# Storing the last tile's 128 results as a column instead of a transposed row

## The chip, the cores and the metric

The kernel runs on one core of a Trainium2 chip. The metric is the device time of one execution in microseconds (us). A second source is the profile: one execution recorded by the hardware profiler, whose span runs from the first to the last recorded instruction.

## The reference

```python
def setup_inputs():
    return {"x": np.random.randn(64, 256, 8192).astype(np.float32)}

def reference(x):
    return np.mean(x, axis=2)
```

The mean over the last axis: 64 x 256 = 16384 rows of 8192 floats each, one result per row. 537 MB are read, 64 KB are written.

## The kernel before, in words

The 16384 rows are seen as 128 tiles of 128 rows (one row to a partition). The first 126 tiles are taken in 63 pairs: partition p of a pair holds two neighbouring rows, 64 KB, in one of three buffers (`bufs`). SyncE's queue (SP) issues all loads: three at the start, then in a loop each as soon as its buffer is free (L108). For each pair VectorE (DVE) sums the first row of each partition into a column of `res0` (L138), and ScalarE (ACT) sums the second row into a column of `res1` (L177).

The last two tiles, T0 and T1, come one by one into the buffer that the loop would use next. T0 is one load (L117); VectorE sums one half, ScalarE the other, and VectorE adds the two halves into `last0` (L145). T1 comes in six chunks of falling size (L119: 4096, 2048, 1024, 512, 256 and 256 columns). Four chunks are halved between VectorE (L148) and ScalarE (L177); VectorE folds the fifth (L153). The sixth lies in a tile `fin` next to the ten partial sums, and one last fold on VectorE (L153, the function `folded`) adds chunk and partial sums, scales by 1/8192 and leaves the 128 finished results of T1 in `last1`, one float on each of 128 partitions. That fold increments `dve_sem` to 3.

The order on each engine is written out by hand, with semaphores between engines. At the end:

- TensorE (PE) transposes `res0` and `res1` through an identity matrix into PSUM (L209, L210). ScalarE copies both, scaled, into `outsb` (L181), and SP stores it (L123).
- TensorE transposes `last0` into `psum_row0`, one row of 128 (L213). ScalarE copies it, scaled, to `row0` (L181, `from_psum`), and SP stores that row of 512 bytes (L126).
- TensorE transposes `last1` into `psum_row1` (L213). VectorE copies it to `row1` (L171), and SP stores this row (L126).
- SP waits for the three stores (L130).

`cp_sem` counts the copies out of PSUM, `pe_sem` the transposes; SP waits for `cp_sem` at 2, 3 and 4 before the three stores.

Of the kernel before, what the change touches and what calls it, by code (L numbers as in the profile page):

```python
# [11 lines left out]
def bass_global_avg_pool_1d_kernel(  # L12
# [4 lines left out]
    P = 128  # L17
# [15 lines left out]
    T0, T1 = 2 * NB, 2 * NB + 1  # L33
    out_flat = out.rearrange("b c -> (b c)")
    out_pairs = out_flat.rearrange("(g q) -> g q", q=2 * P)
    out_tiles = out_flat.rearrange("(t p) -> t p", p=P)
# [11 lines left out]
    with ExitStack() as ctx:  # L48
        sb = lambda n, s: ctx.enter_context(nc.sbuf_tensor(n, s, F32))
        ps = lambda n, s: ctx.enter_context(nc.psum_tensor(n, s, F32))  # L50
        sem = lambda n: ctx.enter_context(nc.semaphore(n))
        half = sb("half", [P, 2])
        last = [sb(f"last{j}", [P, 1]) for j in range(2)]
# [6 lines left out]
        ident = sb("ident", [P, P])  # L60
        outsb = sb("outsb", [NB, 2 * P])
        fin = sb("fin", [P, NFIN])
        added = sb("added", [P, NFIN // 2])
        row = [sb(f"row{j}", [1, P]) for j in range(2)]
        psum = [ps(f"psum{j}", [NB, P]) for j in range(2)]
        psum_row = [ps(f"psum_row{j}", [1, P]) for j in range(2)]
        dve_sem = sem("dve_sem")
        act_sem = sem("act_sem")
        ident_sem = sem("ident_sem")
        pe_sem = sem("pe_sem")  # L70
        cp_sem = sem("cp_sem")
        tile_sem = sem("tile_sem")
        out_sems = [sem(f"out_sem{i}") for i in range(3)]
# [9 lines left out]
        def chunk(c):  # L83
            if c == NCH - 1:
                return fin[:, 0 : ch[c]]
            return tail[:, L + offs[c] : L + offs[c] + ch[c]]


        eng = nc.gpsimd
# [14 lines left out]
        eng = nc.sync  # L104
# [16 lines left out]
            ).then_inc(ch_sems[c], 16)  # L121
        eng.wait_ge(cp_sem, 2)
        eng.dma_start(out_pairs[0:NB, :], outsb[:, :]).then_inc(out_sems[0], 16)  # L123
        for j in range(2):
            eng.wait_ge(cp_sem, 3 + j)
            eng.dma_start(out_tiles[T0 + j : T0 + j + 1, :], row[j][:, :]).then_inc(  # L126
                out_sems[1 + j], 16
            )
        for s in out_sems:
            eng.wait_ge(s, 16)  # L130

# [1 line left out]
        eng = nc.vector  # L133
# [18 lines left out]
        def folded(ap, n, to, scale, done):  # L152
            eng.tensor_tensor_reduce(  # L153
                added[:, 0 : n // 2],
                ap[:, 0 : n // 2],
                ap[:, n // 2 : n],
                scale=scale,
                scalar=0.0,
                op0=ADD,
                op1=ADD,  # L160
                accum_out=to,
            ).then_inc(done, 1)
# [4 lines left out]
        eng.wait_ge(pd_sem, NS + 1)  # L167
        eng.wait_ge(ch_sems[NCH - 1], 16)  # L168
        folded(fin, NFIN, last[1][:], inv, dve_sem)
        eng.wait_ge(pe_sem, 4)  # L170
        eng.tensor_copy(row[1][:, :], psum_row[1][:, :]).then_inc(cp_sem, 1)  # L171


        eng = nc.scalar

        def summed(ap, to, done):
            eng.activation(ap, ap, COPY, accum_out=to).then_inc(done, 1)  # L177

        def from_psum(n, dst, src):
            eng.wait_ge(pe_sem, n)  # L180
            eng.activation(dst, src, COPY, scale=inv).then_inc(cp_sem, 1)  # L181
# [16 lines left out]
        for c in range(NS):  # L198
            eng.wait_ge(ch_sems[c], 16)
            summed(chunk(c)[:, ch[c] // 2 :], part(NS + 1 + c), pa_sem)  # L200
            if c == 0:
                from_psum(3, row[0][:, :], psum_row[0][:, :])


        eng = nc.tensor
# [2 lines left out]
            eng.wait_ge(free_sems[b], 2 * NT)  # L208
        eng.transpose(psum[0][:, :], res[0][:, :], ident[:, :]).then_inc(pe_sem, 1)  # L209
        eng.transpose(psum[1][:, :], res[1][:, :], ident[:, :]).then_inc(pe_sem, 1)  # L210
        for j in range(2):
            eng.wait_ge(dve_sem, 2 + j)
            eng.transpose(psum_row[j][:, :], last[j][:, :], ident[:, :]).then_inc(  # L213
                pe_sem, 1
            )


# [26 lines left out]
```

## Time and profile before

| what | value |
| --- | --- |
| time, median of 3 runs | 1244.41 us (1244.21 to 1244.49) |
| the profiled execution's own time | 1244.37 us |
| its span | 1243.0 us |
| busy: VectorE, ScalarE, TensorE | 557.2, 458.8, 1.4 us |
| DMA queue, share of 16 engines' span | 99.8% |
| read from HBM, mean rate | 536.87 MB, 432 GB/s |
| VectorE's copy of `psum_row1` (L171) | 0.279 us |
| one transpose into `psum_row` (L213) | 0.372 us |

The profiled execution took 1.37 us more than its span; that time lies outside the recorded instructions. Busy times are sums over instructions, and engines work side by side, so they do not add up to the span. The chain that ended last names at each moment what the end was waiting for. Waits of SP are listed on their own.

### The profile page before, as it was taken

Reading aid. Unit: us, or ns where it says so; the run is one execution under the profiler, and the core shown is the slowest. Engines: PE = TensorE matmul, PEld = TensorE weight load, DVE = VectorE, ACT = ScalarE, POOL = GpSimd, SP = SyncE. Lnnn points to the kernel's source line nnn. Section 1 sums busy time; section 2 is a strip of 40 time slices with the busy share of each in tenths; the row PEclk is TensorE's granted clock in tenths of the full one; section 3 lists DMA queues with packets and bytes.
Section 4 is the critical chain, followed back from the end, with each engine's and each line's share of the span. In section 5 each row is a group of like instructions: output and inputs, shape, how many; then the busy total and the mean of one; then the engine's idle time right before and its main releaser. Section 6 shows DMA issues by size and latency. Waiting matters only on the chain.

```text
span 1243.0 us, 887 instructions
## 1 busy us (share of the span) xinstructions
PE 1.4 (0%) x4; PEld 0.4 (0%) x4; DVE 557.2 (45%) x74; ACT 458.8 (37%) x141; POOL 0.7 (0%) x7
## 2 busy tenths in 40 slices
PE   0000000000000000000000000000000000000000
PEld 0000000000000000000000000000000000000000
DVE  2354453543535435344353453544535435354356
ACT  2243242432424424334243342433424324244245
POOL 0000000000000000000000000000000000000000
DMA  9999999999999999999999999999999999999998
GB/s 405 439 439 439 405 439 439 439 439 439 439 422 422 439 439 439 439 439 432 411 439 439 439 439 439 439 426 418 439 439 439 439 439 434 415 432 439 439 439 373
DMA packets 10156, 536.94 MB, mean 432 GB/s; under 512 B 1131, under 2 KB 1452, under 8 KB 1708
## 3 DMA queue, kind: packets, MB, share of 16 engines
q1 hardware_dynamic: 10156, 536.94, 99.8%
HBM read 536.87 MB, written 0.07 MB: 432 GB/s over the span
## 4 chain that ended last, share of the span: by engine, by line
DMA 84%; DVE 15%; issue 0%; SPq 0%; DVEq 0%; PE 0%
DMA buf<-in_x_dram 84%; DVE res L138 15%; SPq L108 0%; DVEq L138 0%; DVE fin L148 0%; SPq L119 0%; DVE added L153 0%; PE psum_row L213 0%; SPq L117 0%; DVE row L171 0%; DVEq L168 0%; DVE fin L153 0%; DVE last L153 0%
## 5 line engine op out<-in xcount | busy, mean ns | idle before, releaser
L138 DVE TENSOR_REDUCE res<-buf 128x8192 f32 x63 | 547.2, 8686 | 682.7 <-DMA buf<-in_x_dram 682.7
L177 ACT ACTIVATE buf<-buf 128x8192 f32<-128x8192 f32 (+2 forms) x68 | 450.5, 6625 | 778.8 <-DMA buf<-in_x_dram 778.7
L177 ACT ACTIVATION_READ_ACCUMULATOR buf<-buf (+1 forms) x68 | 12.6, 186 | 0.0
L142 DVE TENSOR_REDUCE half<-buf 128x1 f32<-128x4096 f32 x1 | 4.4, 4419 | 0.9 <-DMA buf<-in_x_dram 0.9
L148 DVE TENSOR_REDUCE fin<-buf 128x1 f32<-128x2048 f32 (+3 forms) x4 | 4.6, 1153 | 0.3 <-DMA buf<-in_x_dram 0.2
L209 PE MATMUL psum<-ident,res 128*63 128x128 f32 x1 | 0.4, 442 | 1230.1 <-DVE res L138 1230.1
L184 ACT ACT_TABLE_LOAD x1 | 1.3, 1283 | 0.7 <-PEq L229 0.7
L181 ACT ACTIVATE outsb<-psum 63x128 f32<-63x128 f32 x2 | 0.5, 278 | 2.2 <-PE psum L209 2.2
L213 PE MATMUL psum_row<-ident,last 128*1 128x128 f32 x2 | 0.7, 372 | 10.1 <-DVE last L153 5.2
L209 PEld LDWEIGHTS psum<-ident,res 128*63 128x63 f32 x1 | 0.2, 181 | 1230.1 <-issue 1230.1
L171 DVE COPY row<-psum_row 1x128 f32<-1x128 f32 x1 | 0.3, 279 | 0.5 <-PE psum_row L213 0.5
L210 PE MATMUL psum<-ident,res 128*63 128x128 f32 x1 | 0.4, 417 | 0.0
L153 DVE CUSTOM_DVE_ANT_0 added<-fin 128x133 f32<-128x133 f32 x1 | 0.3, 299 | 0.1
L153 DVE CUSTOM_DVE_ANT_0 added<-buf 128x128 f32<-128x128 f32 x1 | 0.3, 293 | 0.0
L93 POOL TENSOR_SCALAR_AFFINE_SELECT ident<-ident 128x128 f32<-128x128 f32 x1 | 0.3, 292 | 0.2 <-POOL ident L91 0.2
L181 ACT ACTIVATE row<-psum_row 1x128 f32<-1x128 f32 x1 | 0.2, 249 | 0.0
L210 PEld LDWEIGHTS psum<-ident,res 128*63 128x63 f32 x1 | 0.2, 231 | 0.0
L184 ACT ACTIVATE warm<-ident 128x1 f32<-128x1 f32 x1 | 0.2, 203 | 0.0
L91 POOL MEMSET ident<- 128x128 f32 x1 | 0.2, 204 | 0.0
L145 DVE TENSOR_REDUCE last<-half 128x1 f32<-128x2 f32 x1 | 0.2, 155 | 0.1
L213 PEld LDWEIGHTS psum_row<-ident,last 128*1 128x1 f32 x2 | 0.2, 79 | 10.8 <-DVE last L153 5.5
L229 POOL MEMSET const-bfloat16-1.0<- 128x1 bf16 x1 | 0.1, 101 | 0.0
(6 smaller groups left out, 0.6 us busy)
## 6 DMA issues: line engine op xcount, KB each, us to landing
buf<-in_x_dram SPq DMA_DIRECT2D x1, 4096.0 KB, 39.5
buf<-in_x_dram SPq DMA_DIRECT2D x1, 2048.0 KB, 43.9
buf<-in_x_dram SPq DMA_DIRECT2D x1, 1024.0 KB, 45.9
buf<-in_x_dram SPq DMA_DIRECT2D x63, 49.0
buf<-in_x_dram SPq DMA_DIRECT2D x1, 512.0 KB, 46.7
buf<-in_x_dram SPq DMA_DIRECT2D x1, 256.0 KB, 46.9
buf<-in_x_dram SPq DMA_DIRECT2D x1, 128.0 KB, 46.8
fin<-in_x_dram SPq DMA_DIRECT2D x1, 128.0 KB, 46.6
```

The source lines that it names most:

```text
L93: eng.affine_select(out=ident[:], in_=ident[:], compare_op=mybir.AluOpType.not_equal, fill=1.0, base=0, pattern=[[-1, P]], channel_multipl ...
L138: eng.tensor_reduce(res[0][:, bass.ds(NBUF * i + b, 1)], bufs[b][:, 0:L], X, ADD).then_inc(free_sems[b], 1)
L142: eng.tensor_reduce(half[:, 0:1], tile0[:, 0:H], X, ADD).then_inc(dve_sem, 1)
L148: eng.tensor_reduce(part(c), chunk(c)[:, 0 : ch[c] // 2], X, ADD).then_inc(pd_sem, 1)
L153: eng.tensor_tensor_reduce(added[:, 0 : n // 2], ap[:, 0 : n // 2], ap[:, n // 2 : n], scale=scale, scalar=0.0, op0=ADD, op1=ADD, accum_ou ...
L171: eng.tensor_copy(row[1][:, :], psum_row[1][:, :]).then_inc(cp_sem, 1)
L177: eng.activation(ap, ap, COPY, accum_out=to).then_inc(done, 1)
L181: eng.activation(dst, src, COPY, scale=inv).then_inc(cp_sem, 1)
L184: eng.activation(warm[:], ident[:, 0:1], COPY)
L209: eng.transpose(psum[0][:, :], res[0][:, :], ident[:, :]).then_inc(pe_sem, 1)
L210: eng.transpose(psum[1][:, :], res[1][:, :], ident[:, :]).then_inc(pe_sem, 1)
L213: eng.transpose(psum_row[j][:, :], last[j][:, :], ident[:, :]).then_inc(pe_sem, 1)
```

## The change

The 128 results of T1 are no longer transposed. SP waits for the last fold (`dve_sem` at 3) and stores `last1` as it lies: 128 partitions of one float each go to 128 consecutive floats of the output, in one DMA. The transpose of `last1`, the PSUM tile and the row tile for it, and VectorE's copy go. T0 is handled as before.

```diff
-        row = [sb(f"row{j}", [1, P]) for j in range(2)]
+        row = sb("row", [1, P])
-        psum_row = [ps(f"psum_row{j}", [1, P]) for j in range(2)]
+        psum_row = ps("psum_row", [1, P])
...
         eng.wait_ge(cp_sem, 2)
         eng.dma_start(out_pairs[0:NB, :], outsb[:, :]).then_inc(out_sems[0], 16)
-        for j in range(2):
-            eng.wait_ge(cp_sem, 3 + j)
-            eng.dma_start(out_tiles[T0 + j : T0 + j + 1, :], row[j][:, :]).then_inc(
-                out_sems[1 + j], 16
-            )
+        eng.wait_ge(cp_sem, 3)
+        eng.dma_start(out_tiles[T0 : T0 + 1, :], row[:, :]).then_inc(out_sems[1], 16)
+
+        eng.wait_ge(dve_sem, 3)
+        eng.dma_start(
+            out_tiles[T1].rearrange("(p o) -> p o", o=1), last[1][:]
+        ).then_inc(out_sems[2], 16)
         for s in out_sems:
             eng.wait_ge(s, 16)
...
         folded(fin, NFIN, last[1][:], inv, dve_sem)
-        eng.wait_ge(pe_sem, 4)
-        eng.tensor_copy(row[1][:, :], psum_row[1][:, :]).then_inc(cp_sem, 1)
...
-                from_psum(3, row[0][:, :], psum_row[0][:, :])
+                from_psum(3, row[:, :], psum_row[:, :])
...
-        for j in range(2):
-            eng.wait_ge(dve_sem, 2 + j)
-            eng.transpose(psum_row[j][:, :], last[j][:, :], ident[:, :]).then_inc(
-                pe_sem, 1
-            )
+        eng.wait_ge(dve_sem, 2)
+        eng.transpose(psum_row[:, :], last[0][:, :], ident[:, :]).then_inc(pe_sem, 1)
```

## The prediction

> **What bounds the kernel now.** The page comes first: the span, the DMA rows, and the chain that ended last.
>
> ```profile
> span 1243.0 us, 887 instructions
> ...
> DMA packets 10156, 536.94 MB, mean 432 GB/s; under 512 B 1131, under 2 KB 1452, under 8 KB 1708
> ...
> q1 hardware_dynamic: 10156, 536.94, 99.8%
> ...
> DMA 84%; DVE 15%; issue 0%; SPq 0%; DVEq 0%; PE 0%
> ```
>
> The one DMA queue is busy for 99.8% of the span and moves 432 GB/s: loading x is the kernel. The change touches no load, so it acts only after the last load has landed. The chain of waits from the end of VectorE's last fold on is:
>
> ```profile
> 1241.15 0.02 DVE last L153
> 1241.17 0.04 issue
> 1241.21 0.39 PE psum_row L213
> 1241.60 0.02 issue
> 1241.62 0.28 DVE row L171
> ```
>
> It is a strict sequence. VectorE's last fold ends at 1241.17, TensorE transposes from 1241.21 to 1241.60, VectorE copies from 1241.62 to 1241.90. The timeline and the waits of the SP queue give the rest:
>
> ```profile
> 1241.93 0.23 SPq L126 DMA_DIRECT2D out_dram<-row  x1
> ```
>
> ```profile
> SPq L130 <- DMA out_dram<-row: 0.8, 1, 0.8
> ```
>
> The store of the last row is issued from 1241.93 to 1242.16, and SP then waits 0.8 us for it: 1243.0 − 1241.93 = 1.07 us from the start of the issue to the end of the span. Where those 1.07 us lie, and how a DMA of 128 rows looks when the queue is empty, is seen by cutting the span into windows around the first load (issued at 0.75) and around this store:
>
> ```profile
> core 0: us, PE busy (x) PEld busy (x) DVE busy (x) ACT busy (x) POOL busy (x), PEclk, DMA share, GB/s
> ...
> 1.17:1.79 0.62, 0.00 (x0) 0.00 (x0) 0.00 (x0) 0.62 (x1) 0.29 (x1) 1.00 0.00 0
> 1.79:1.85 0.06, 0.00 (x0) 0.00 (x0) 0.00 (x0) 0.06 (x1) 0.00 (x0) 1.00 16.12 5461
> 1.85:2.00 0.15, 0.00 (x0) 0.00 (x0) 0.00 (x0) 0.15 (x1) 0.00 (x0) 1.00 9.28 3058
> 2.00:2.25 0.25, 0.00 (x0) 0.00 (x0) 0.00 (x0) 0.23 (x2) 0.00 (x0) 1.00 2.39 786
> 2.25:2.31 0.06, 0.00 (x0) 0.00 (x0) 0.00 (x0) 0.00 (x0) 0.00 (x0) 1.00 3.00 1092
> ...
> 1242.16:1242.62 0.46, 0.00 (x0) 0.00 (x0) 0.00 (x0) 0.00 (x0) 0.00 (x0) 1.00 0.00 0
> 1242.62:1242.69 0.07, 0.00 (x0) 0.00 (x0) 0.00 (x0) 0.00 (x0) 0.00 (x0) 1.00 0.03 7
> 1242.69:1243.00 0.31, 0.00 (x0) 0.00 (x0) 0.00 (x0) 0.00 (x0) 0.00 (x0) 1.00 0.00 0
> ```
>
> A packet's bytes are booked where it starts, which is why shares exceed 1 here. GB/s times window gives 328, 459, 197 and 66 KB; a row of this load is 65.5 KB, so that is 5, 7, 3 and 1 packets, together one for each of the 16 engines. They start between 1.79 and 2.31: 1.04 to 1.56 us after the issue began. The one-row store at the end has its only packets 0.69 us after its issue began, in a window that holds 0.03 x 0.07 us x 16 = 34 ns of packet time (the 512 bytes and one small packet), and then 0.31 us pass until the span is over.
>
> **What is removed.** The transpose (0.39 us with its start), the copy (0.28 us) and two hand-overs (0.04 and 0.02 us) leave the path. By the instruction lists of both kernels nothing else moves: one TensorE matmul with its weight load and one VectorE copy are gone; SP keeps three stores, the last with another source. The fold of VectorE ends at 1241.17 as before, and a hand-over from VectorE to SP took 0.03 us (copy ends 1241.90, issue starts 1241.93). So the last store begins at 1241.20 instead of 1241.93: −0.73 us. No other engine's work is uncovered, since nothing runs beside this chain: ScalarE's last instruction ended at 1240.57 (timeline), and the two earlier stores were issued at 1231.08 and 1237.90.
>
> **What is added: the wait.** SP now waits for the fold itself. Queued behind this wait are only the store and the three final waits; the row of tile T0 was released at 1237.90, long before. It costs nothing more.
>
> **What is added: the store of 128 times 4 bytes.** It takes the place of one 512-byte row. Three terms:
>
> 1. The start. No store of 128 rows stands in this trace. The nearest rows are the one-row store (packet at 0.69 us) and the first load, of 128 rows (last engine at 1.56 us). The low end is the difference of the issues alone: the first loop load's issue row L108 has a median of 0.333 us, this store 0.227 us, so +0.11 us. The high end is the whole difference, 1.56 − 0.69 = +0.87 us. I take the high end, because the column has the partition count of the load and the queue is empty in both cases; against it, the load is the first DMA of the program.
> 2. The packets. By the page there are 70 loads and 3 stores, and 1131 packets below 512 B. 70 x 16 = 1120 of them belong to loads, which leaves 11 for the stores. As a load of 128 rows has 16, I expect the column to have 128 data packets and 16 small ones, eight data packets to an engine. Price of one: the 34 ns are for a data packet and a small one together, so 34 ns is generous for a packet of 4 bytes. Low end: eight at nothing. I take seven more than the one row had: 7 x 34 = 0.24 us. High end: each write waits until the one before is through, priced with the 0.31 us that follow the packets of the row: 7 x 0.31 = 2.17 us. The row nearest to it is the packet's own time, since the loads' packets follow each other on an engine without such a pause (the queue's 99.8%).
> 3. The end, from the last packet to SP's release: 0.31 us, as before.
>
> The Trainium skill speaks against this change: "DMA: Bandwidth & Descriptors", Specifications, says that a transfer below 512 B is done as a read and a modified write back. It gives no time for that. "HBM Reference", Latency, gives 0.2 us for one access, so an estimate of a read and a write in turn for eight packets of an engine is 8 x 0.4 = 3.2 us, and the sum would be −0.73 + 0.87 + 3.2 = +3.3 us. No trace here shows a store below 512 B; the row that goes furthest in this direction is the 0.31 us above.
>
> **Sum.** −0.73 + 0.87 + 0.24 = +0.38 us: the span becomes 1243.4. The profiled execution took 1244.37 us, 1.37 more than its span, which I leave as it is: 1244.75. The median of the runs is 1244.41, 0.04 above the profiled one, and they spread over 0.28 us; I round to 1244.7. Low ends together: −0.73 + 0.11 = −0.62, which is 1243.75. High ends together: −0.73 + 0.87 + 2.17 = +2.31, which is 1246.7.
>
> A measurement of this kernel can tell about 0.2% from no change, that is 2.49 us, from 1241.9 to 1246.9. All of these ends lie inside.
>
> **Rivals.**
>
> *Slower: the writes to one half-kilobyte do not overlap.* All 128 results go to the same 512 bytes of HBM, from 16 engines. If the memory takes such writes one at a time, it is 128 and not 8 in a row. At 34 ns each that is 4.35 us from the first packet on, 1.04 us after the issue began: −0.73 + (1.04 − 0.69) + 4.35 − 0.03 = +3.94 us, or 1248.3. It decides from the point where 128 packets take 2.49 + 0.73 − 0.35 + 0.03 = 2.90 us, at 22.7 ns each. For it speaks that no row of this trace has several writers in the same bytes; against it, that the packet time in the row is that of an engine and covers 512 bytes. Chance 0.15, with everything else that makes single small writes dearer than the high end.
>
> *The start of 16 engines costs only the issue.* If the spread from 1.79 to 2.31 belongs to the first DMA of a program, terms 1 and 2 are near their low ends: −0.62 + at most 0.24, so 1243.8 to 1244.0. For it speaks that the first load meets an empty chip; against, that its 1.04 us to the first packet are 0.35 later than the row's while the issue is only 0.11 longer. Still no change that can be told. Chance 0.15.
>
> *Faster by over 0.2%.* The windows show the load's last packets before 1240.5; from there to the end are 2.5 us, of which the final folds and any store must stay. A gain of 2.49 us would need a store for nothing, or another rate in the loads, which are the same instructions. Chance 0.02.
>
> *That the change does not do what it says* is ruled out by the instruction lists.
>
> **Chances.** Forecast 0.68, cheap start 0.15, serial writes 0.15, faster 0.02. Within 0.2%: 0.68 + 0.15 = 0.83; slower 0.15; faster 0.02. The range goes from the low ends, 1243.7, to the high ends, 1246.7, and 0.1 for the spread of the runs: 1246.8. It leaves out the serial writes and the gain, 0.17.
>
> **What would show it.** Right: the page of after has 10156 − 2 + 144 = 10298 packets, 1131 − 1 + 128 + 16 = 1274 of them under 512 B; no L171 copy and one psum_row matmul fewer; the last store's issue starts 0.03 us after the fold, and is 0.3 to 0.4 us long; from its start to the end of the span lie 1.9 to 2.3 us in place of 1.07. Term 1 is wrong if the packets start less than 1 us after the issue; term 2, if they are spread over much more than 0.8 us. The forecast falls if the span is over 1245.5, or if the last load packets end at another time than 1240.4.

## The result and the profile after

The changed kernel takes 1249.99 us (median of 6 runs, 1249.41 to 1250.58) against 1244.22 of the kernel before in the same comparison (1243.88 to 1244.49). The ratio is 1.0047, with a 95% interval of 1.0036 to 1.0058: 5.8 us slower, more than the 0.2% that can be told. The profiled execution took 1250.07 us, its span is 1248.7.

The page of the changed kernel, its span and its DMA packets:

```profile
span 1248.7 us, 884 instructions
...
DMA packets 10298, 536.94 MB, mean 430 GB/s; under 512 B 1274, under 2 KB 1594, under 8 KB 1850
```

Packets are what was expected to the last one: 10298, and 1274 below 512 B. The instructions are three fewer, 884 for 887: by the two pages one TensorE matmul with its weight load and one VectorE copy. The timeline of the changed kernel's end (start, duration, what):

```profile
1240.73 0.30 DVE L155 CUSTOM_DVE_ANT_0 added<-fin 128x133 f32<-128x133 f32 x1
1240.96 0.08 DVE L155 DVE_READ_ACCUMULATOR2_ANT last<- 128x1 f32 x1
1241.07 0.37 SPq L128 DMA_DIRECT2D out_dram<-last  x1
```

The fold ends at 1241.04 and the store is issued 0.03 us later, so the transpose and the copy are off the path as planned. The waits of SP in the changed kernel, and the same end cut into windows (columns as in the prediction's windows; the last two are DMA share and GB/s):

```profile
SPq L132 <- DMA out_dram<-last: 7.2, 1, 7.2
```

```profile
1241.44:1241.91 0.47, 0.00 (x0) 0.00 (x0) 0.00 (x0) 0.00 (x0) 0.00 (x0) 1.00 0.00 0
1241.91:1242.13 0.22, 0.00 (x0) 0.00 (x0) 0.00 (x0) 0.00 (x0) 0.00 (x0) 1.00 0.35 3
1242.13:1248.70 6.57, 0.00 (x0) 0.00 (x0) 0.00 (x0) 0.00 (x0) 0.00 (x0) 1.00 0.00 0
```

All 144 packets start within 0.22 us, the first of them 0.84 us after the issue began. Then for 6.57 us no engine and no DMA packet is at work, and SP waits. Where the row of before needed 0.31 us from its last packet to SP's release, the column needs 6.57.

The last load lands at slightly different times from run to run, so kernels are best compared by the tail, from the end of the last fold to the end of the span: 1243.0 − 1241.17 = 1.83 us before, 1248.7 − 1241.04 = 7.66 after. The difference, 5.83, is the whole of the 5.8 us.

### The profile page after: what moved, and what is told of

Same layout as the page of the kernel before. It is cut to its first block, busy times and chain, and to the rows that moved or that the text cites. A ratio compares the mean times of both kernels' runs of the same rounds, so it can differ in the third digit from the quotient of the medians.

```text
span 1248.7 us, 884 instructions
## 1 busy us (share of the span) xinstructions
PE 1.0 (0%) x3; PEld 0.4 (0%) x3; DVE 556.9 (45%) x73; ACT 458.8 (37%) x141; POOL 0.7 (0%) x7
## 2 busy tenths in 40 slices
DMA packets 10298, 536.94 MB, mean 430 GB/s; under 512 B 1274, under 2 KB 1594, under 8 KB 1850
## 3 DMA queue, kind: packets, MB, share of 16 engines
q1 hardware_dynamic: 10298, 536.94, 99.4%
## 4 chain that ended last, share of the span: by engine, by line
DMA 84%; DVE 15%; issue 0%; SPq 0%; DVEq 0%
DMA buf<-in_x_dram 84%; DVE res L140 15%; DVE fin L150 0%; SPq L108 0%; DVEq L140 0%; DVE added L155 0%; SPq L119 0%; SPq L117 0%; DVEq L170 0%; DVE fin L155 0%; DVE last L155 0%
```

## Experiments

### Where the wait comes from: a row of stores, one after another

Behind the three stores of the changed kernel further stores follow, each with a semaphore of its own. `col(n, s)` stands for n floats of the output, s floats from one to the next; `...` marks what is left out:

```diff
         for s in out_sems:
             eng.wait_ge(s, 16)
+        ...
+        eng.dma_start(col(P, 1), last[1][:]).then_inc(more[1], 16)
+        eng.wait_ge(more[1], 16)
+        eng.dma_start(col(64, 1), last[1][0:64, :]).then_inc(more[2], 16)
+        eng.wait_ge(more[2], 16)
+        ...
+        eng.dma_start(col(P, 8), last[1][:], ...).then_inc(more[7], 16)
+        eng.wait_ge(more[7], 16)
+        ...
```

> The changed kernel, and behind its end a row of further stores into the output, each waited for before the next, so that each has a wait of its own on SP (the outputs are stored again at the end). The column store of the changed kernel waited 7.2 us after its issue, 6.57 us of it after its last packet. Theory A, the memory takes small writes into the same stretch of bytes one after another (6.57 us / 128 = 51 ns each): 64, 32 and 16 results wait about 3.9, 2.3 and 1.4 us; 127 results wait about as long as 128, whichever engines carry them; 128 results 512 B apart fall to 1 to 2 us, and the distance at which they fall shows the stretch. Theory B, each engine waits for each of its eight writes (0.82 us each), wherever they go: 512 B apart stays at 7 us, 16 results wait about 1.4 us, 64 about 3.9. Theory C, a store of partial lines has one fixed price: 16 results and 1 result wait about 7 us too. Theory D, the reading of 128 partitions is slow, not the writing: 512 B apart stays at 7 us, and so does 128 x 64 B. All: one row waits 0.8 us, the load of 128 x 4 B under 2 us except by D.

The waits of SP in this kernel; a wait stands under the line of the store that follows it, so L149 is the wait for the column of 128 issued at L146, L152 for the 64 results of L149, L164 for the 127 of L161, L170 for the 128 of L167 that lie 64 bytes apart, and L215 for the last column of the kernel:

```profile
SPq L164 <- DMA out_dram<-last: 9.7, 1, 9.7
SPq L215 <- DMA out_dram<-last: 7.5, 1, 7.5
SPq L152 <- DMA out_dram<-last: 7.4, 1, 7.4
SPq L149 <- DMA out_dram<-last: 7.4, 1, 7.4
...
SPq L170 <- DMA out_dram<-last: 1.1, 1, 1.1
```

All waits of this first row of stores, in us after the issue: one row of 512 B 0.8; 1 result 0.8; 16 results 2.3; 32 results 4.1; 64 results 7.4; 128 results 6.8 to 7.5; 127 results 9.7. With 32, 64, 128, 256 or 512 bytes from one result to the next, 128 results wait 1.1 each time. 128 pieces of 8 B wait 2.8, of 32 to 256 B 1.1, of 512 B 1.2. The load of 128 times 4 B waits 1.6.

Theories B, C and D fall: 128 packets of 4 bytes from the same 128 partitions wait 1.1 us once their targets lie apart, and a single result waits 0.8. Theory A stands in kind, the address decides. Its size was off: 64 results wait as long as 128, not half.

### How far the stretch reaches

> A second row of stores behind the end of the changed kernel, each waited for by itself (outputs are stored again at the end). Theory A2: writes into the same 32 bytes get in each other's way, at about 0.1 us a write, and all such writes of one stretch of 256 bytes go one after another, while two stretches go at once. Then 64 results in bytes 128 to 384 wait about 4 us, as 32 did, in place of 7.4; 32 results in bytes 192 to 320 wait about 2.3, as 16 did; 96 wait about 7.4; 48 about 5.5; 128 results 8 B apart about 2.8, as 128 x 8 B did; 16 B apart between 1.1 and 2.8; 127 results 32 B apart on one engine under 2.5 us in place of 9.7. Rival A3, no stretches but a limit on how many such writes are under way: 64 results wait 7.4 us wherever they lie. Rival B, each engine waits for its own writes: 127 results on one engine wait 9.7 us at 32 B apart too. The column into SBUF waits about 1 us if HBM sets the price, about 7 if the engines do. 4 x 128 B wait about 0.9.

The waits of SP in this kernel, again under the line of the next store: L149 is 64 results in bytes 0 to 256, L152 is 64 in bytes 128 to 384, L191 is 127 results 32 B apart, L197 is the column into SBUF. A stretch of 256 bytes is counted from the start of the output.

```profile
SPq L149 <- DMA out_dram<-last: 8.0, 1, 8.0
...
SPq L152 <- DMA out_dram<-last: 4.1, 1, 4.1
...
SPq L191 <- DMA out_dram<-last: 2.4, 1, 2.4
...
SPq L197 <- DMA line<-last: 1.4, 1, 1.4
```

The same 64 packets wait 8.0 us inside one stretch of 256 bytes and 4.1 when they lie half in one and half in the next; 32 results wait 4.2 inside one and 2.1 across two. So two stretches are served at once, and rival A3 (a limit on writes under way) falls. For 127 results the trace holds 127 + 1 packets, started over 0.75 us, where 128 results have 128 + 16 in 0.2 us: one small packet for sixteen, which we read as one engine for sixteen. They wait 9.8 us next to each other and 2.4 at 32 B apart, so an engine by itself does not wait for each of its writes. Into SBUF the column waits 1.4 us, though its 512 bytes are adjacent there too: the price is on HBM's side. Four points miss: 128 results 8 B apart waited 4.0 in place of 2.8; 48 results waited 6.7 in place of 5.5; 96 waited 5.9 in place of 7.4, less than 48; and eight results in 32 bytes waited 1.0, with no price at all, which "the same 32 bytes" cannot explain. A column of 128 at another place in the output waited 7.5, as before.

### Thirty-two bytes, or how many to a stretch of 256

> A third row of stores behind the end of the changed kernel. Until now eight results into one stretch of 32 bytes waited 1.0 us, as long as ones that lie apart, while 16, 32 and 48 in one stretch of 256 bytes waited 2.2, 4.2 and 6.7; 128 results 32 B apart are eight to 256 bytes and waited 1.1. Theory N, the price goes by how many of these writes fall into one stretch of 256 bytes, and the first eight are free: 16 in bytes 224 to 288 wait about 1 us (eight in each stretch), 16 results 8 or 16 B apart wait 2.2 as 16 next to each other do, 32 results 8 B apart wait about 4, 32 results 16 B apart about 2. Theory G, the price goes by writes into the same 32 bytes: 16 in bytes 224 to 288 wait 2.2 as at 0 to 64, 16 results 16 B apart (two to 32 bytes) wait about 1. Both: 16 and 32 results 32 B apart wait about 1 us.

The waits of SP, L157 for 16 results in bytes 128 to 192 and L160 for 16 in bytes 224 to 288:

```profile
SPq L157 <- DMA out_dram<-last: 2.3, 1, 2.3
...
SPq L160 <- DMA out_dram<-last: 1.0, 1, 1.0
```

Eight and twelve results wait 0.9 us. Sixteen in one stretch of 256 bytes wait 1.6 and 2.3 next to each other, 2.3 at 8 B, 1.8 at 16 B and 1.3 at 32 B apart. Thirty-two results wait 3.9 next to each other, 5.0 at 8 B apart (one stretch), 2.0 at 16 B (two stretches) and 1.0 at 32 B (four). That is theory N in its main lines, and against theory G: 16 results two to 32 bytes wait 1.8, and 16 across the border of two stretches 1.0. Theory N also accounts for a miss of the row before: 128 results 8 B apart are 32 to a stretch, and they waited 4.0, about as long as 32 next to each other. It is no exact law. That 96 waited less than 48 does not follow from it. Thirty-two across the border waited 1.0 here and 2.1 in the row before, and 128 next to each other 6.6 to 8.5 in one execution. Only one border, at byte 256 of the output, was tried. What happens inside the memory is left open.

### In the kernel: the column spread out

```diff
+        eng.wait_ge(out_sems[0], 16)
+        eng.wait_ge(out_sems[1], 16)
         eng.wait_ge(dve_sem, 3)
         eng.dma_start(
-            out_tiles[T1].rearrange("(p o) -> p o", o=1), last[1][:]
+            out_flat[0 : 8 * P].rearrange("(p s) -> p s", s=8)[:, 0:1],
+            last[1][:],
+            allow_slow_non_contiguous=True,
         ).then_inc(out_sems[2], 16)
```

> The changed kernel with one thing changed: T1's 128 results are stored 32 bytes apart instead of 4 (so they stand in the places of other rows' results and T1's own places stay empty; the store also waits for the two earlier stores, which land before 1240.8). Theory that the price is many writers in the same 32 bytes: the wait after the issue falls from 7.2 to about 1.1 us as it did in the row of stores, the span is about 0.5 us below that of before, the time 0.3 to 0.6 us below before. Theory that the price is 128 small packets whatever their addresses (or that a store at the end of a kernel is dear): the time stays 5.5 to 6 us above before.

1243.72 us against 1244.19, ratio 0.9997 (0.9988 to 1.0006). The end of the fold (from the chain that ended last) and the wait of SP in this kernel:

```profile
1240.84 0.01 DVE last L159
```

```profile
SPq L136 <- DMA out_dram<-last: 1.0, 1, 1.0
```

The 5.8 us are gone. Two things changed in the kernel: the addresses, 4 bytes apart or 32, and the two added waits for the earlier stores. The waits are not the reason, since in the rows of stores the column waited for all stores before it and still took 6.8 to 7.5 us. The sixteen increments of the store's semaphore in the two traces show the same: with adjacent addresses they arrive one by one from 1244.8 to 1248.7, with addresses 32 B apart all from 1242.2 to 1242.4. The tail is 1242.4 − 1240.85 = 1.55 us, 0.28 below that of before; in the time that gain can't be told, since the interval includes 1.

### In the kernel: the removal alone

```diff
         eng.wait_ge(dve_sem, 3)
-        eng.dma_start(
-            out_tiles[T1].rearrange("(p o) -> p o", o=1), last[1][:]
-        ).then_inc(out_sems[2], 16)
+        eng.dma_start(out_tiles[T1 : T1 + 1, :], row[:, :]).then_inc(out_sems[2], 16)
```

> The removal alone: the changed kernel, where the store that waits for T1's fold sends the ready row of T0 (512 bytes in one piece) instead of the column, so T1's places get T0's results. What is taken off the path is the transpose, the copy and two hand-overs, nothing is added: 0.73 us below before by the chain of before. If the removal has a hidden cost, the gain is smaller or none.

1243.38 us against 1244.19, ratio 0.9993 (0.9984 to 1.0002). The end of the fold and the wait of SP:

```profile
1240.66 0.01 DVE last L153
```

```profile
SPq L130 <- DMA out_dram<-row: 0.8, 1, 0.8
```

The tail is 1241.8 − 1240.67 = 1.13 us, 0.70 below before, where 0.73 was expected. In the tail the removal is worth what the chain said. In the time it can't be told: 0.73 us are 0.06%, and the interval includes 1.

### In the kernel: T0 as the column instead of T1

T0's `last0` is scaled by ScalarE into `col0` and stored as a column; T1 goes through transpose and copy as before. The changed counts of `pe_sem` are left out here.

```diff
-                from_psum(3, row[0][:, :], psum_row[0][:, :])
+                eng.wait_ge(dve_sem, 2)
+                eng.activation(col0[:], last[0][:], COPY, scale=inv).then_inc(cp_sem, 1)
...
-        for j in range(2):
-            eng.wait_ge(cp_sem, 3 + j)
-            eng.dma_start(out_tiles[T0 + j : T0 + j + 1, :], row[j][:, :]).then_inc(
-                out_sems[1 + j], 16
-            )
+        eng.wait_ge(cp_sem, 3)
+        eng.dma_start(
+            out_tiles[T0].rearrange("(p o) -> p o", o=1), col0[:]
+        ).then_inc(out_sems[1], 16)
+        eng.wait_ge(cp_sem, 4)
+        eng.dma_start(out_tiles[T1 : T1 + 1, :], row[1][:, :]).then_inc(out_sems[2], 16)
```

> The kernel before with T0 stored as a column and T1 as the transposed row. T0's store is issued at 1237.9, 4 us before T1's. Theory that the column is hidden there: the time stays that of before, 1244.4. Theory A to D, with its packets queued behind the last loads until about 1240.4 as the row's were: its landing ends 6.8 us later, near 1247.2, so about 1248.6 in time, 4 us over before and 1.4 under the changed kernel; the loads and folds keep their times.

1247.07 us against 1244.13, ratio 1.0023 (1.0013 to 1.0032). The wait of SP at the end, and the time from the column's issue (at 1237.69) to its landing:

```profile
SPq L132 <- DMA out_dram<-col: 4.2, 1, 4.2
```

```profile
out_dram<-col SPq DMA_DIRECT2D x1, 0.5 KB, 8.5
```

Issued 4 us earlier, the column is still not hidden: its increments arrive from 1240.7 to 1246.2, after the last loads. The price is smaller than the 4 us that were expected, 2.9; the landing ended 1 us earlier than was expected from the lone column, and why is open.

### A version without transpose on TensorE and without the column

VectorE transposes T1's results in blocks of 32 x 32 in SBUF (`sq` is a zeroed tile whose first column the fold fills), and SP stores four pieces of 128 bytes. The lines that zero `sq` are left out here.

```diff
-        folded(fin, NFIN, last[1][:], inv, dve_sem)
+        folded(fin, NFIN, sq[:, 0:1], inv, dve_sem)
+        eng.wait_ge(dve_sem, 3)
+        eng.transpose(sqt[:], sq[:]).then_inc(dve_sem, 1)
...
-        eng.wait_ge(dve_sem, 3)
+        eng.wait_ge(dve_sem, 4)
         eng.dma_start(
-            out_tiles[T1].rearrange("(p o) -> p o", o=1), last[1][:]
+            out_tiles[T1].rearrange("(p w) -> p w", w=32), sqt[0:P:32, :]
         ).then_inc(out_sems[2], 16)
```

> A version that keeps the removal and avoids the column: VectorE transposes T1's results in blocks of 32 x 32 within SBUF, and four pieces of 128 bytes are stored in one DMA. Off the path are the 0.73 us of transpose, copy and hand-overs; on it come a hand-over on VectorE and the block transpose, 0.2 to 0.35 us by the small VectorE instructions of the trace (0.1 to 0.3 us each), and about 0.15 us of the store (its wait was 0.9 in place of 0.8, its issue 0.05 longer). By theories that put the price in the writes to the same 32 bytes: 0.2 to 0.4 us below before. By theories that put it in stores from several partitions as such: above before.

1244.11 us against 1244.19, ratio 0.9999 (0.9990 to 1.0008): no difference. The timeline of this kernel:

```profile
1240.46 0.21 DVE L176 STREAM_TRANSPOSE sqt<-sq 128x32 f32<-128x32 f32 x1
1240.70 0.62 SPq L131 DMA_DIRECT2D out_dram<-sqt  x1
```

The block transpose took 0.21 us and the wait 0.9, as expected, but the issue took 0.62 us and not about 0.28. The expected 0.2 to 0.4 us did not come, and that is what they went into: the tail is 1242.4 − 1240.44 = 1.96 us, 0.13 above that of before. In the rows of stores four pieces from partitions 0 to 3 were issued in 0.27 us, four from partitions 0, 32, 64 and 96 in 0.61.

## Why the prediction was wrong, point by point

**What bounds the kernel, and the removal: right.** The change acted only behind the last load. The store began 0.03 us after the fold, and the removal by itself shortened the tail by 0.70 us (0.73 in the sum).

**The start (term 1): too dear, on the wrong row.** 0.87 us was the step from the row's packet to the last late start in the first load. After the change all packets had started 0.84 to 1.06 us after the issue began, and "less than 1 us" was the prediction's own sign that the term is wrong. Counted to the end of the packets, where the 0.31 us of term 3 begin, the row of before needed 0.76 us (1242.69 − 1241.93) and the column 1.06. So terms 1 and 2 together are +0.30 us, where the sum had 1.11; 0.14 of the 0.30 are the longer issue (0.37 for 0.23 us).

The prediction named the first DMA of a program as a possible reason for the late starts of the load. The runs speak against it. In the first row of stores a load of 128 times 4 B comes at the end of the program, when the queue is empty (its issue, then the windows around it):

```profile
1302.34 0.34 SPq L200 DMA_DIRECT2D fin<-in_x_dram  x1
```

```profile
1302.30:1303.29 0.99, 0.00 (x0) 0.00 (x0) 0.00 (x0) 0.00 (x0) 0.00 (x0) 1.00 0.00 0
1303.29:1303.50 0.21, 0.00 (x0) 0.00 (x0) 0.00 (x0) 0.00 (x0) 0.00 (x0) 1.00 0.07 1
1303.50:1303.75 0.25, 0.00 (x0) 0.00 (x0) 0.00 (x0) 0.00 (x0) 0.00 (x0) 1.00 0.11 1
1303.75:1304.00 0.25, 0.00 (x0) 0.00 (x0) 0.00 (x0) 0.00 (x0) 0.00 (x0) 1.00 0.09 1
1304.00:1304.30 0.30, 0.00 (x0) 0.00 (x0) 0.00 (x0) 0.00 (x0) 0.00 (x0) 1.00 0.00 0
```

Its packets start 0.95 to 1.66 us after the issue began, about as late and as spread out as the first load's 1.04 to 1.56. So the mistake was to price a store by a load; why the loads start later is open.

**The packets (term 2): about right, and beside the point.** The 144 packets started within 0.22 us; the term was 0.24.

**The end (term 3): this is the step that failed.** "0.31 us, as before" measured 6.57 us, an error of 6.26. The 0.31 us were taken from a store with one writer and carried to one with 128 writers in two stretches of 256 bytes. It got no bounds of its own, though no row of before showed several writers close together; the only bound for dear writes was hung on term 2 and spread over engines (7 x 0.31 us), and 127 writes through one engine waited only 2.4 us once they lay 32 B apart. With the parts that the two profiles measured, the sum is −0.73 + 0.30 + 6.26 = +5.83 us, for 5.8 measured. From the start of the issue to the end of the span lay 7.63 us, where the prediction's signs had 1.9 to 2.3.

**The rivals.** "The writes to one half-kilobyte do not overlap" was the right mechanism in kind, with a chance of 0.15. Its price was 34 ns each, from a packet's time, which gave 1248.3; it is 6.57 us / 128 = 51 ns on average, and by the experiments rather 64 in each of two stretches at once, about 0.1 us each (6.57 / 64). "The start of 16 engines costs only the issue" had terms 1 and 2 at 0.11 to 0.35 us, and 0.30 was measured; the reason that it gave, the first DMA of a program, does not hold, and its time was wrong with term 3. The range ended at 1246.8 because it left out the serial writes, the one rival that no row of before could test.

**The rule on small transfers.** The Trainium skill, "DMA: Bandwidth & Descriptors", Specifications, has a transfer below 512 B done as a read and a modified write. No run here shows whether a small store is done so. The runs show that such stores can be dear, but not by their size alone: 128 pieces of 4 B waited 1.1 us at 32 B apart, as 128 pieces of 32 to 256 B did and 0.1 less than 128 of 512 B. Dear were only many pieces within the same 256 bytes. The prediction's estimate from the pages, +3.3 us, was nearer than its own sum, but by luck: it lets the eight writes of an engine wait for one another, and the engine is not where the wait arises.

## What to carry to other kernels

A store of one float per partition into adjacent addresses is many writers in a few hundred bytes of HBM; here that cost over 6 us after the last packet, more than a transpose, a PSUM copy and one contiguous row together (0.73 + 1.07 us). Issuing it 4 us earlier did not hide it while it queued behind loads: 2.9 us of it were left. When a store at the end of a kernel changes shape, price the wait for its completion anew, from a row with as many writers to the same bytes, and if there is none let the range hold that case.

## What the runs showed of the hardware

- Stores of 4-byte pieces into one stretch of 256 bytes next to each other waited 0.9 to 1.0 us for 8 or 12 pieces, 1.6 to 2.3 for 16, 3.9 to 4.2 for 32, 6.7 for 48 and 6.9 to 8.1 for 64. Laid across the border of two stretches they waited about half, or less (64: 3.7 and 4.1).
- The price does not show in the DMA share or in packet times (in the changed kernel 0.35 x 0.22 us x 16 / 144 = 8.6 ns a packet), only in the wait for the semaphore.
- A DMA that reads four partitions 32 apart was issued in 0.61 us, from four neighbouring ones in 0.27. The step is not all that sets this time: stores of 64 neighbouring results took 0.47 to 0.55 us to issue, of 128 results 0.33 to 0.37.
